# Routing gates of a 16,384-expert layer: one-hot products on TensorE, or accumulating scatters into DRAM

## The chip, the cores and the metric

The kernel runs on one core of one Trainium2 chip. The metric is the device time of one launch in microseconds (us); of several runs the median is taken. Five engines take part: TensorE (PE in the tables, with its weight loads as PEld), VectorE (DVE), ScalarE (ACT), GpSimd (POOL) and SyncE (SP), and 16 DMA engines that move data for all of them. SP, ACT and POOL issue the DMAs.

## The reference, cut to what matters

Two transformer blocks are computed for 256 tokens of width 1024 in float32. The last part is a PEER feed-forward layer: 8 heads, each of which picks 16 of 16,384 experts for each token by a top-16 of two half scores and a top-16 of their 256 sums.

```python
def peer_ffn(xn, w_q, sub_keys, expert_u, expert_v):
    q = (xn @ w_q).reshape(B, S, PEER_HEADS, 2, PEER_QDIM // 2)
    s = jnp.einsum('bshpd,hpkd->bshpk', q, sub_keys)
    v_half, i_half = lax.top_k(s, PEER_TOPK)
    cand = v_half[..., 0, :, None] + v_half[..., 1, None, :]
    top_s, top_c = lax.top_k(cand.reshape(B, S, PEER_HEADS, PEER_TOPK * PEER_TOPK), PEER_TOPK)
    i1 = jnp.take_along_axis(i_half[..., 0, :], top_c // PEER_TOPK, axis=-1)
    i2 = jnp.take_along_axis(i_half[..., 1, :], top_c % PEER_TOPK, axis=-1)
    experts = i1 * PEER_NKEYS + i2
    g = jax.nn.softmax(top_s.astype(jnp.float32), axis=-1)
    ...
        u = expert_u[ec]
        act = jax.nn.gelu(jnp.einsum('cd,ced->ce', xc, u).astype(jnp.float32))
        return jnp.einsum('ce,ced->cd', gc * act, expert_v[ec])
```

Both kernels compute this densely: the activation of every expert for every token, times a dense gate matrix that is zero where an expert was not picked, times all of `expert_v`. Two heads of a token can pick the same expert; their gates add up.

## The kernel before, in words

**The two blocks up to the layer.** Weights come in as 512 KB tiles over SP's queue (`wtile`, lines 236 to 247, four buffers `wf`). A float32 product is done as three products of rounded halves, so each tile is split by ACT (the high part `wh`) and DVE (the low part `wl`). The second block's attention loops over two token tiles `tt` and four head pairs `j` (lines 880 to 909). Then come its output product, a norm, the query product `wq` and the scores `sco` (lines 1010 to 1021). Up to there a planner orders the instructions.

**The u phase (lines 1136 to 1168).** From line 1023 on the order is the program's. The 16,384 experts are 128 columns `i2` of 128 experts. For each of the first `NS` = 122 columns a tile of `expert_u` is loaded by SP (`u_load`), split (`u_low`) and multiplied with the tokens (`u_mm`: 24 products of 256 columns on PE). ACT applies the gelu into one of two buffers (`u_act`) and writes the 128 KB to DRAM (`act_d`, line 1142).

**The routing.** Between the columns DVE does the top-16 steps of `route`, once for each token tile with all 8 heads. The loop keeps two counters of planned DVE and PE time: each column adds 1.2 to DVE's and 2.9 to PE's, and routing steps run while DVE's is the smaller.

**The gates.** When a token tile is routed, PE transposes its indices and gates (`turn`, line 1084). Then for each 4 tokens `g_prep` makes two one-hot tiles on DVE and ACT, `g_mm` multiplies them on PE (line 1120, four products of 128 columns) and `g_evac` copies the result into `gb`, 8 MB for each token tile, on chip (line 1125). That is 64 groups.

**The v phase (lines 1172 to 1255).** The six remaining columns of `expert_u` and the 128 tiles of `expert_v` share one list of jobs. POOL loads the stored activations back, two columns at a time (`act_load`, line 1196), DVE multiplies them with `gb` (line 1205), the product is split, and PE does 12 products of 512 columns for each column (`v_mm`). The tail adds the residual and the last norm.

Of the kernel before, what the change touches and what calls it, by code (L numbers as in the profile page):

```python
# [19 lines left out]
P = 128  # L20
# [12 lines left out]
C_IOTA = C_SIN + 32  # L33
C_I16 = C_IOTA + 128
# [12 lines left out]
def _consts():  # L47
# [12 lines left out]
    c[:, C_IOTA:C_IOTA + P] = np.arange(P)[None, :]  # L60
# [92 lines left out]
def tile_block(ctx, tc, d, out, NS=122, CONV="0.2 0.2 1.1 1.1 1.2", K1=4, M0=7, MR=65, ML=8, MQ=40, WB=3, NTAIL=2, WARM=7):  # L153
# [57 lines left out]
    gt_d = dram.tile([2, D], F32, name="gt_d")  # L211
    cB = xp.tile([P, D], F32, name="cB")
# [475 lines left out]


    with ExitStack() as sb:  # L690
# [4 lines left out]
        cw2 = pb.tile([P, 256], F32, name="cw2")  # L695

# [180 lines left out]
        for tt in range(NT):  # L877
# [3 lines left out]
            for j in range(4):  # L881
# [80 lines left out]
    with ExitStack() as sc_:  # L962
        pc = sc_.enter_context(tc.tile_pool(name="pc", bufs=1))
        act_d = dram.tile([P, P, S], F32, name="act_d")
        iT = pc.tile([P, 2, S], F32, name="iT")
        gT = pc.tile([P, S], F32, name="gT")
        gb = [pc.tile([P, P, P], F32, name="gb0"), None]
        sg_ = ExitStack()
        so = ExitStack()
        po_ = so.enter_context(tc.tile_pool(name="poh", bufs=1, side="right"))  # L970

        def u_prep(i2, lo_eng):
            return wtile(d["u"][i2].rearrange("p a b -> p (a b)"), lo_eng=lo_eng)

        def u_load(i2):
            f = wp.tile([P, 1024], F32, name=nm("wf"), tag="wf", bufs=4)
            nc.sync.dma_start(f, d["u"][i2].rearrange("p a b -> p (a b)"))
# [19 lines left out]
        def u_act(p):  # L997
            a_ = pc.tile([P, S], F32, name=nm("act"), tag="act", bufs=2)
            A.activation(a_, p, AF.Gelu_apprx_tanh)  # L999
            return a_  # L1000
# [23 lines left out]
        i16 = cst[:, C_I16:C_I16 + 16]  # L1024

# [8 lines left out]
        def route(tt, res):  # L1034

            vals = rk.tile([P, 8, 2, 16], F32, name=nm("vals"), tag="vals", bufs=1)
            idx = rk.tile([P, 8, 2, 16], U32, name=nm("idx"), tag="idx", bufs=1)

            def half(h, p_):
                top16(sco[:, tt, h, p_, :], vals[:, h, p_, :], idx[:, h, p_, :], "mr", P)  # L1040

            tv = rk.tile([P, 8, 16], F32, name=nm("tv"), tag="tv")
            ti = rk.tile([P, 8, 16], U32, name=nm("ti"), tag="ti", bufs=1)

            def both(h):
                cand = rk.tile([P, 16, 16], F32, name=nm("cand"), tag="cand")
                V.tensor_tensor(cand, vals[:, h, 0, :, None].to_broadcast([P, 16, 16]),
                                vals[:, h, 1, None, :].to_broadcast([P, 16, 16]), op=OP.add)
                top16(cand.rearrange("p a b -> p (a b)"), tv[:, h, :], ti[:, h, :], "mc", S)

            te = rk.tile([P, 8, 16], F32, name=nm("te"), tag="te")
            idf = rk.tile([P, 8, 2, 16], F32, name=nm("idf"), tag="idf", bufs=1)
            abf = rk.tile([P, 2, 8, 16], F32, name=nm("abf"), tag="abf", bufs=1)
            sel = rk.tile([P, 3, 8, 16], F32, name=nm("sel"), tag="sel")

            def places():
                V.tensor_tensor(te, tv, tv[:, :, 0:1].to_broadcast([P, 8, 16]), op=OP.subtract)
                V.tensor_copy(idf, idx)
                ab = rk.tile([P, 2, 8, 16], U32, name=nm("ab"), tag="ab", bufs=1)
                V.tensor_scalar(ab[:, 0], ti, 4, None, op0=OP.logical_shift_right)  # L1060
                V.tensor_scalar(ab[:, 1], ti, 15, None, op0=OP.bitwise_and)
                V.tensor_copy(abf, ab)
                later.append(lambda: A.activation(te, te, AF.Exp))

            def pick(p_, h4):
                h_ = slice(4 * h4, 4 * h4 + 4)
                e_ = rk.tile([P, 4, 16, 16], F32, name=nm("eq"), tag="eq")
                V.tensor_tensor(e_, abf[:, p_, h_, :, None].to_broadcast([P, 4, 16, 16]),
                                i16[:, None, None, :].to_broadcast([P, 4, 16, 16]), op=OP.is_equal)
                V.tensor_tensor(e_, e_, idf[:, h_, p_, None, :].to_broadcast([P, 4, 16, 16]), op=OP.mult)  # L1070
                V.tensor_reduce(sel[:, p_, h_, :], e_, axis=AX.X, op=OP.add)

            def share():
                zs = rk.tile([P, 8], F32, name=nm("zs"), tag="zs")
                V.tensor_reduce(zs, te, axis=AX.X, op=OP.add)
                V.reciprocal(zs, zs)
                V.tensor_tensor(sel[:, 2], te, zs[:, :, None].to_broadcast([P, 8, 16]), op=OP.mult)
                later.append(turn)

            def turn():  # L1080
                t_ = slice(tt * P, tt * P + P)
                t = gp()[:, 0:384].rearrange("p (i t) -> p i t", i=3)
                for i in range(3):
                    T.transpose(t[:, i, :], sel[:, i].rearrange("p h s -> p (h s)"), ident)
                A.activation(iT[:, :, t_], t[:, 0:2], AF.Copy)
                A.activation(gT[:, t_], t[:, 2, :], AF.Copy)
                res.append(tt)

            for h in range(8):
                for p_ in range(2):  # L1090
                    yield 1.57, lambda h=h, p_=p_: half(h, p_)
            for h in range(8):
                yield 2.75, lambda h=h: both(h)
            yield 1.4, places
            for p_ in range(2):
                for h4 in range(2):
                    yield 3.5, lambda p_=p_, h4=h4: pick(p_, h4)
            yield 0.8, share


        iota = cst[:, C_IOTA:C_IOTA + P]

        def g_prep(t4, mul):

            t_ = slice(4 * t4, 4 * t4 + 4)
            oh = [po_.tile([P, 4, P], F32, name=nm("oh"), tag=f"oh{i}", bufs=2) for i in range(2)]
            for i, o in enumerate(oh):
                V.tensor_tensor(o, iota[:, None, :].to_broadcast([P, 4, P]),
                                iT[:, i, t_, None].to_broadcast([P, 4, P]), op=OP.is_equal)
            if mul is V:  # L1110
                V.tensor_tensor(oh[1], oh[1], gT[:, t_, None].to_broadcast([P, 4, P]), op=OP.mult)
            else:
                for q_ in range(4):
                    A.activation(oh[1][:, q_, :], oh[1][:, q_, :], AF.Copy, scale=gT[:, 4 * t4 + q_:4 * t4 + q_ + 1])
            later.append(lambda: g_mm(t4, oh))

        def g_mm(t4, oh):
            pt = ga_().rearrange("p (t i) -> p t i", t=4)
            for q_ in range(4):
                T.matmul(pt[:, q_, :], oh[0][:, q_, :], oh[1][:, q_, :], start=True, stop=True)  # L1120
            later.append(lambda: g_evac(t4, pt))

        def g_evac(t4, pt):
            tt, o = divmod(4 * t4, P)
            A.activation(gb[tt][:, :, o:o + 4], pt.rearrange("p t i -> p i t"), AF.Copy)


        prep = [u_prep(0, V), u_prep(1, V)]
        later, done = [], []
        gens = iter([route(tt, done) for tt in range(NT)])  # L1130
        cur = next(gens)
        nxt = next(cur)
        g_left = list(range(S // 4))
        dve, pe = 0.0, 0.0
        p = None
        for i in range(NS):
# [11 lines left out]
            if nxt is None and sr is not None and len(done) == NT:  # L1148
                sr.close()
                sr = None  # L1150
                pg1 = sg_.enter_context(tc.tile_pool(name="pg1", bufs=1))
                gb[1] = pg1.tile([P, P, P], F32, name="gb1")

            for n in range(2):
# [161 lines left out]
```

## Time and profile before

| | |
|---|---|
| median of 3 runs | 1244.12 us (1240.11 to 1595.06) |
| the profiled execution | 1238.48 us, span 1236.7 us, mean granted TensorE clock 0.992 |
| PE busy | 1200.8 us, 97% |
| DVE busy | 950.3 us, 77% |
| ACT busy | 699.0 us, 57% |
| POOL busy | 87.6 us, 7% |
| DMA | 264.05 MB, mean 214 GB/s |

The span runs from the first to the last instruction. A busy engine is one with an instruction in flight; products on PE are pipelined, so the busy times of lines can overlap. "Granted clock" is the share of TensorE's full speed.

### The profile page before, as it was taken

The page shows a single profiled execution, that of the slowest core. Times are in us where ns is not written, and L with a number is a line of the kernel's source. Part 1 is how long each engine was busy: PE and PEld are TensorE (multiplying, and loading weights), DVE is VectorE, ACT ScalarE, POOL GpSimd, SP SyncE. Part 2 cuts the span into 40 slices and gives each one's busy share as a digit, 9 for nine tenths or more (in the row PEclk, how much of TensorE's full clock was granted, in tenths as well). Part 3 has the DMA queues.
Part 4 walks back from the last instruction along what each step waited for, and adds up shares of the span by engine and source line. Part 5 has one row for each costly group of instructions (what it writes and reads, how often), then busy time and mean ns, then how long its engine had stood idle before and what let it go on. Part 6 is the DMA issues. An engine that isn't in the chain of part 4 may idle for free.

```text
span 1236.7 us, 20785 instructions
## 1 busy us (share of the span) xinstructions
PE 1200.8 (97%) x7541; PEld 1069.1 (86%) x7541; DVE 950.3 (77%) x1911; ACT 699.0 (57%) x1267; POOL 87.6 (7%) x118
## 2 busy tenths in 40 slices
PE   8999999979988999999999999999999999999996
PEld 7777887879987999999999999999888888888885
DVE  5886969876678589989999899546777777767766
ACT  6566544574455555558878477645444444445443
POOL 2001100010101000000000000000111110101102
PEclk9999999989999999999999999999999999999999
DMA  8876888746523757655555644777776776777764
GB/s 285 301 240 223 292 240 320 262 144 230 187 87 73 251 169 223 224 196 175 182 177 179 208 147 142 230 232 224 242 237 223 238 232 230 230 232 229 241 212 152
DMA packets 86279, 264.05 MB, mean 214 GB/s; under 512 B 10253, under 2 KB 26389, under 8 KB 85664
## 3 DMA queue, kind: packets, MB, share of 16 engines
q1 hardware_dynamic: 62352, 225.03, 55.6%
q0 software_dynamic: 5680, 19.48, 5.0%
q10 hardware_dynamic: 18144, 18.23, 4.2%
q8 instruction: 59, 0.97, 0.3%
q14 instruction: 44, 0.36, 0.1%
HBM read 244.58 MB, written 19.68 MB: 214 GB/s over the span
## 4 chain that ended last, share of the span: by engine, by line
PE 79%; issue 7%; DVE 7%; DMA 3%; ACT 2%; POOL 1%; SPq 0%; ACTq 0%; POOLq 0%; DVEq 0%
PE sc L994 9%; PE sc L992 9%; PE sc L993 9%; PE po L1230 5%; PE pg L1230 5%; PE po L1229 5%; PE po L1231 5%; PE pg L1229 5%; PE pg L1231 5%; PE pg L1120 5%; PE pg L257 3%; PE pg L258 3%; PE pg L256 3%; DVE wl L231 2%; DMA wf<-in_w_br_dram 2%
## 5 line engine op out<-in xcount | busy, mean ns | idle before, releaser
L231 DVE TENSOR_TENSOR wl<-wf,wh 128x1024 fp32r<-128x1024 f32 (+3 forms) x255 | 302.5, 1189 | 131.7 <-ACT wh L230 131.3
L230 ACT ACTIVATE wh<-wf 128x1024 fp32r<-128x1024 f32 (+3 forms) x255 | 260.1, 1022 | 119.4 <-PE pg L258 49.2
L992 PE MATMUL sc<-hThi,wh 128*128 128x256 f32 x1024 | 293.8, 287 | 0.0
L994 PE MATMUL sc<-hThi,wl 128*128 128x256 f32 x1024 | 290.7, 284 | 2.3 <-DVE wl L984 2.3
L993 PE MATMUL sc<-hTlo,wh 128*128 128x256 f32 x1024 | 289.5, 283 | 0.0
L994 PEld LDWEIGHTS sc<-hThi,wl 128*128 128x128 f32 x1024 | 196.0, 191 | 3.8 <-DVE wl L984 2.9
L993 PEld LDWEIGHTS sc<-hTlo,wh 128*128 128x128 f32 x1024 | 196.3, 192 | 0.2
L992 PEld LDWEIGHTS sc<-hThi,wh 128*128 128x128 f32 x1024 | 196.1, 192 | 0.2
L984 DVE TENSOR_TENSOR wl<-wf,wh 128x1024 fp32r<-128x1024 f32 x122 | 147.7, 1217 | 49.4 <-ACT wh L979 48.7
L230 ACT ACTIVATE wwh<-w 128x256 fp32r<-128x256 f32 x128 | 53.4, 417 | 170.7 <-issue 147.6
L979 ACT ACTIVATE wh<-wf 128x1024 fp32r<-128x1024 f32 x122 | 128.9, 1057 | 31.5 <-ACT act L999 18.6
L256 PE MATMUL pg<-wh,hThi 128*128 128x512 f32 (+1 forms) x264 | 102.2, 388 | 1.9 <-ACT hThi L323 1.9
L257 PE MATMUL pg<-wl,hThi 128*128 128x512 f32 (+1 forms) x264 | 102.6, 389 | 0.4 <-DVE wl L231 0.4
L1230 PE MATMUL po<-wl,wwh 128*128 128x512 f32 x256 | 102.1, 399 | 0.0
L1230 PE MATMUL pg<-wl,wwh 128*128 128x512 f32 x256 | 102.1, 399 | 0.0
L258 PE MATMUL pg<-wh,hTlo 128*128 128x512 f32 (+1 forms) x264 | 102.1, 388 | 0.0
L1229 PE MATMUL po<-wh,wwh 128*128 128x512 f32 x256 | 100.9, 394 | 0.0
L1229 PE MATMUL pg<-wh,wwh 128*128 128x512 f32 x256 | 100.9, 394 | 0.0
L1231 PE MATMUL po<-wh,wwl 128*128 128x512 f32 x256 | 100.4, 392 | 0.0
L1231 PE MATMUL pg<-wh,wwl 128*128 128x512 f32 x256 | 100.3, 392 | 0.0
L1196 POOL DMA_DIRECT2D actl<-act_d x61 | 44.2, 725 | 746.4 <-ACT act L999 378.9
L999 ACT ACTIVATE act<-sc 128x256 f32<-128x256 f32 x128 | 48.1, 376 | 75.8 <-PE sc L994 71.8
(375 smaller groups left out, 2122.4 us busy)
## 6 DMA issues: line engine op xcount, KB each, us to landing
wf<-in_u_dram SPq DMA_DIRECT2D x128, 512.0 KB, 3.8
wf<-in_v_dram SPq DMA_DIRECT2D x128, 512.0 KB, 4.2
wf<-in_w_in_dram SPq DMA_DIRECT2D x68, 512.0 KB, 5.2
wm<-in_w_mod_dram SPq DMA_DIRECT2D x48, 512.0 KB, 6.1
act_d<-act ACTq DMA_DIRECT2D x122, 128.0 KB, 3.3
actl<-act_d POOLq DMA_DIRECT2D x61, 256.0 KB, 4.3
wf<-in_w_out_dram SPq DMA_DIRECT2D x16, 512.0 KB, 4.8
wf<-in_w_br_dram SPq DMA_DIRECT2D x8, 512.0 KB, 10.5
```

Source lines behind the costliest of these rows:

```text
L230: A.activation(hi, src, AF.Copy)
L231: (lo_eng or V).tensor_tensor(lo, src, hi.bitcast(F32), op=OP.subtract)
L256: T.matmul(p, lh[:, k, t], hh, start=first, stop=False)
L257: T.matmul(p, lh[:, k, t], l_, start=False, stop=False)
L258: T.matmul(p, ll[:, k, t], hh, start=False, stop=last)
L984: V.tensor_tensor(l, f, h.bitcast(F32), op=OP.subtract)
L992: T.matmul(p, h[:, o], hThi[:, k, :], start=(k == 0), stop=False)
L993: T.matmul(p, h[:, o], hTlo[:, k, :], start=False, stop=False)
L994: T.matmul(p, l[:, o], hThi[:, k, :], start=False, stop=(k == KD - 1))
L1229: T.matmul(pO[tt][n], wh[:, t_], h[:, c_], start=first, stop=False)
L1230: T.matmul(pO[tt][n], wh[:, t_], l[:, c_], start=False, stop=False)
L1231: T.matmul(pO[tt][n], wl[:, t_], h[:, c_], start=False, stop=last)
```

## The change

The dense gate matrix moves from the chip to DRAM, and the activations from DRAM to the chip.

- A DRAM tensor `g_d` of 128 x 128 x 256 floats (16.8 MB) is filled with zeros by 32 writes of 512 KB on ACT's queue, four after each `j` step of the second block's attention.
- The routing goes by groups of heads, (0), (1), (2, 3), (4, 5), (6, 7), both token tiles in a group. At the end of a group the cell numbers are computed, and for each row (a head and a token tile) POOL issues 16 indirect DMAs, each of which adds 128 gates of 4 bytes, one for each token, into `g_d`. The first transfer of a row waits until the 16 of the same token tile one head earlier have landed; nothing else orders them. That is 256 transfers.
- `g_prep`, `g_mm`, `g_evac`, `turn` and `act_d` are gone. The gelu writes into activations that stay on chip, 80 columns in one tile and 48 in a second, made where the routing's buffers were. All 128 columns of `expert_u` run in the u phase.
- When the routing is over, POOL queues loads of the gates, two columns (256 KB) at a time, three buffers. The first waits until the transfers of the last head have landed. `w_make` multiplies activations and gates, one DVE instruction for 256 tokens instead of two for 128. `w_make(0)` stands in the u phase ahead of the split of the tile that is loaded at column 126.

```diff
+    g_d = dram.tile([P, P, S], F32, name="g_d")
+    g_flat = g_d.rearrange("i p (t o) -> (i p t) o", o=1)
...
+    def zero_gates(zero, n):
+        return nc.scalar.dma_start(g_d.rearrange("i p t -> i (p t)")[:, 1024 * n:1024 * n + 1024].rearrange("i (a b) -> i a b", b=512),
+                            zero[:, None, :].to_broadcast([P, 2, 512]))
...
                 for k, at in enumerate(CONV.split()):
                     if at == f"{tt}.{j}":
                         conv[k]()
+                for n in range(4):
+                    tc.keep_in_program_order(zero_gates(zero, 16 * tt + 4 * j + n))
...
+        acts = [pc.tile([P, NA, S], F32, name="act0"), None]
+        ixr = pc.tile([P, 16, 16], U32, name="ixr")
+        gtr = pc.tile([P, 16, 16], F32, name="gtr")
...
-        for tt in range(NT):
-            for h2 in range(4):
+        for h2 in range(4):
+            for tt in range(NT):
...
-        man = sc_.enter_context(tc.manual_schedule())
+        man = sc_.enter_context(tc.manual_schedule(engines={getattr(mybir.EngineType, e) for e in ("PE", "DVE", "Activation", "SP")}))
...
+        def scatter(r):
+            h, tt = divmod(r, NT)
+            for j in range(16):
+                q_ = nc.gpsimd.indirect_dma_start(g_flat, bass.IndirectOffsetOnAxis(ap=ixr[:, r, j:j + 1], axis=0),
+                                                  gtr[:, r, j:j + 1], None, compute_op=OP.add)
+                prev = scat.get(r - NT, []) if j == 0 else []
+                for o_ in prev:
+                    tc.add_manual_dep(q_.ins, o_.name, mybir.DependencyInfo(mybir.DependencyClass.Sync,
+                                                                        mybir.DependencyReason.DATA),
+                                      reason="a head after the one before")
+                tc.declare_no_dep(q_.ins, group="scat", keep=prev, reason="other cells, or a later wait")
...
+            def cells():
+                f = rk.tile([P, 4, 16], F32, name=nm("cf"), tag="cf")
+                V.scalar_tensor_tensor(f[:, :n], sel[:, 1, :n], float(P * S), tok[:, :n, None].to_broadcast([P, n, 16]),
+                                       op0=OP.mult, op1=OP.add)
+                V.scalar_tensor_tensor(ixr[:, R], sel[:, 0, :n], float(S), f[:, :n], op0=OP.mult, op1=OP.add)
 
             def share():
...
-                later.append(turn)
-
-            def turn():
...
+                for r in range(r0, r0 + n):
+                    scatter(r)
...
-        def g_prep(t4, mul):
...
-        def g_mm(t4, oh):
...
-        def g_evac(t4, pt):
...
+        steps = (st_ for heads in ((0,), (1,), (2, 3), (4, 5), (6, 7)) for st_ in route(heads))
...
+        def g_load():
+            if g_todo:
+                i2 = g_todo.pop(0)
+                g_ = pw.tile([P, 2, S], F32, name=nm("gl"), tag="gl", bufs=3)
+                q_ = nc.gpsimd.dma_start(g_, g_d[i2:i2 + 2].rearrange("i p t -> p i t"))
+                if i2 == 0:
+                    for r in (14, 15):
+                        for o_ in scat[r]:
...
+                                              reason="all gates are in")
...
+        def w_make(i2):
+            w = pw.tile([P, S], F32, name=nm("w"), tag="w", bufs=2)
+            V.tensor_tensor(w, act_of(i2), gls.pop(i2), op=OP.mult)
+            if i2 % 2:
+                g_load()
...
+        for i in range(P):
             now, later = later, []
             q = p
             p = u_mm(*prep.pop(0))
             if q is not None:
-                nc.scalar.dma_start(act_d[i - 1], u_act(q))
+                A.activation(act_of(i - 1), q, AF.Gelu_apprx_tanh)
...
+            if i == P - 2:
+                w_make(0)
...
             prep.append(u_low(*h))
+            if nxt is None and pw is None:
+                sr.close()
+                pa_ = sg_.enter_context(tc.tile_pool(name="pa1", bufs=1))
+                acts[1] = pa_.tile([P, P - NA, S], F32, name="act1")
+                pw = sg_.enter_context(tc.tile_pool(name="pw", bufs=1, side="right"))
+                for _ in range(3):
+                    g_load()
+        A.activation(act_of(P - 1), p, AF.Gelu_apprx_tanh)
+        w_make(1)
...
+        for i in range(P):
             h, l = prep.pop(0)
-            if kind == "u":
-                acts[i2] = u_act(u_mm(h, l))
-                continue
...
+            if i + 2 < P:
+                w_make(i + 2)
+                prep.append(u_low(*u_load(P + i + 2)))
```

## Rows read from the trace of the kernel before

**Rows 1.** First parts of the page: busy time of each engine, and PE in 40 slices.

```profile
PE 1200.8 (97%) x7541; PEld 1069.1 (86%) x7541; DVE 950.3 (77%) x1911; ACT 699.0 (57%) x1267; POOL 87.6 (7%) x118
PE   8999999979988999999999999999999999999996
```

**Rows 2.** Windows: length; busy us of PE, PEld, DVE, ACT, POOL; clock, DMA share, GB/s.

```profile
460.00:480.00 20.00, 20.00 (x169) 20.00 (x168) 18.92 (x66) 10.11 (x14) 0.00 (x0) 1.00 0.72 226
500.00:550.00 50.00, 49.10 (x408) 48.68 (x407) 43.99 (x68) 26.19 (x37) 0.00 (x0) 1.00 0.67 223
650.00:700.00 50.00, 49.14 (x412) 48.72 (x410) 47.40 (x71) 34.24 (x61) 0.00 (x0) 1.00 0.61 194
800.00:850.00 50.00, 50.00 (x419) 50.00 (x418) 21.20 (x18) 25.14 (x35) 0.00 (x0) 1.00 0.77 230
900.00:1000.00 100.00, 100.00 (x442) 81.01 (x441) 72.58 (x141) 48.92 (x72) 12.31 (x17) 1.00 0.72 232
```

**Rows 3.** Chain that ended last, in the u phase: start, length, what.

```profile
548.93 1.29 DVE oh L1108 x2
...
628.07 0.89 PE pg L1120 x8
631.83 0.89 PE pg L1120 x8
...
775.00 1.78 PE pg L1120 x16
779.65 1.78 PE pg L1120 x16
```

**Rows 4.** Lines L1142, L1120, L1084: shortest/median/longest ns, first and last start.

```profile
L1142 ACTq DMA_DIRECT2D act_d<-act x121: 326/327/362, 440.6 to 848.1; - x121
L1120 PE MATMUL pg<-oh,oh x512: 270/275/347, 551.2 to 781.2; 128*128 128x128 f32 x171
L1084 PE MATMUL pg<-cst,sel x6: 270/272/272, 548.0 to 706.3; 128*128 128x128 f32 x6
```

**Rows 5.** Groups of POOL by line and form: busy us, mean ns of one, idle before.

```profile
L1196 POOL DMA_DIRECT2D actl<-act_d x61 | 44.2, 725 | 746.4 <-ACT act L999 378.9 <-DVE w L1205 286.1 <-DMA wf<-in_v_dram 68.3
L371 POOL DMA_DIRECT2D gt_d<-modc x2 | 1.9, 964 | 34.4 <-DVE modc L366 34.4
L499 POOL DMA_DIRECT2D rel<-in_rel_dram x1 | 0.5, 545 | 0.0
```

**Rows 6.** DMA issues over the whole span: count, KB each, median us to landing.

```profile
wf<-in_u_dram SPq DMA_DIRECT2D x128, 512.0 KB, 3.8
actl<-act_d POOLq DMA_DIRECT2D x61, 256.0 KB, 4.3
gt_d<-modc POOLq DMA_DIRECT2D x2, 4.0 KB, 10.8
e<-e__989 POOLq DMA_DIRECT2D x1, 12.0 KB, 2.8
```

**Rows 7.** DMA totals of the stretches 170:178, 397:400, 400:403 and 181:184.

```profile
DMA packets 181, 0.60 MB, mean 75 GB/s; under 512 B 35, under 2 KB 35, under 8 KB 181
...
DMA packets 20, 0.08 MB, mean 27 GB/s; under 512 B 0, under 2 KB 0, under 8 KB 20
...
DMA packets 22, 0.09 MB, mean 30 GB/s; under 512 B 0, under 2 KB 0, under 8 KB 22
...
DMA packets 332, 1.27 MB, mean 422 GB/s; under 512 B 23, under 2 KB 23, under 8 KB 332
```

**Rows 8.** DMAs issued between 397 and 400: count, KB each, median us to landing.

```profile
wf<-in_wq_dram SPq DMA_DIRECT2D x1, 512.0 KB, 10.3
```

**Rows 9.** Window of the second block's attention, columns as in the windows above.

```profile
340.00:400.00 60.00, 54.06 (x351) 47.03 (x349) 46.51 (x109) 31.57 (x75) 4.77 (x9) 1.00 0.30 82
```

More of the change, by code (lines that the diff above doesn't have):

```diff
@@ L695, in tile_block @@
         cw2 = pb.tile([P, 256], F32, name="cw2")
+        zero = pb.tile([P, 512], F32, name="zero")
+        G.memset(zero, 0.0)
         def proj_T(ci, consume):
@@ L995, in u_mm, with act_of @@
             return p
[L997 to L1000, printed above, removed]
+        def act_of(i2):
+            return acts[0][:, i2, :] if i2 < NA else acts[1][:, i2 - NA, :]
         sr = ExitStack()
@@ L1090, in route @@
                 for p_ in range(2):
[L1091 to L1094, printed above, removed]
+                    yield 1.57, lambda r=r, p_=p_: half(r, p_)
+            for r in range(n):
+                yield 2.75, lambda r=r: both(r)
+            yield 1.2, places
             for p_ in range(2):
-                for h4 in range(2):
-                    yield 3.5, lambda p_=p_, h4=h4: pick(p_, h4)
+                yield 0.9 * n, lambda p_=p_: pick(p_)
@@ L1098, in route @@
+            yield 0.5, cells
             yield 0.8, share
-        iota = cst[:, C_IOTA:C_IOTA + P]
-        def g_prep(t4, mul):
[L1105 to L1115, printed above, removed]
@@ L1131, in tile_block @@
-        cur = next(gens)
-        nxt = next(cur)
-        g_left = list(range(S // 4))
+        prep = [u_low(*u_load(0)), u_low(*u_load(1))]
+        steps = (st_ for heads in ((0,), (1,), (2, 3), (4, 5), (6, 7)) for st_ in route(heads))
+        nxt = next(steps)
         dve, pe = 0.0, 0.0
         p = None
-        for i in range(NS):
+        gls, g_todo = {}, list(range(0, P, 2))
+        pw = None
+        wts = {}
+        def g_load():
[6 more added lines that the diff above has]
+                        for o_ in scat[r]:
+                            tc.add_manual_dep(q_.ins, o_.name, mybir.DependencyInfo(mybir.DependencyClass.Sync,
+                                                                                mybir.DependencyReason.DATA),
+                                              reason="all gates are in")
+                    keep = [o_ for r in (14, 15) for o_ in scat[r]]
+                else:
+                    keep = []
+                tc.declare_no_dep(q_.ins, group="scat", keep=keep, reason="the first load waited for all")
+                tc.stamp_issue_order_token(q_.ins, "gates")
+                gls[i2], gls[i2 + 1] = g_[:, 0, :], g_[:, 1, :]
@@ L1138, in tile_block @@
+        def w_make(i2):
[3 more added lines that the diff above has]
+                g_load()
+            wh = pw.tile([P, S], F32R, name=nm("wwh"), tag="wwh", bufs=4)
+            wl = pw.tile([P, S], F32R, name=nm("wwl"), tag="wwl", bufs=4)
+            split(w, wh, wl)
+            wts[i2] = (wh, wl)
+        for i in range(P):
             now, later = later, []
@@ L1147, in tile_block @@
             pe += 2.9
[L1148 to L1154, printed above, removed]
-                if g_left and gb[g_left[0] // 32] is not None and g_left[0] // 32 in done and (n == 0 or nxt is None):
-                    g_prep(g_left.pop(0), V if n else A)
-                    dve += 1.8 if n else 1.2
-                    pe += 0.88
+            if i == P - 2:
+                w_make(0)
             while nxt is not None and dve < pe:
@@ L1161, in tile_block @@
                 nxt[1]()
-                nxt = next(cur, None)
-                if nxt is None:
-                    cur = next(gens, None)
-                    nxt = next(cur) if cur else None
+                nxt = next(steps, None)
             prep.append(u_low(*h))
-        nc.scalar.dma_start(act_d[NS - 1], u_act(p))
-        assert not g_left and not later
-        so.close()
-        pO = [[op_(), op_()], [gp(), gp()]]
-        pw = sg_.enter_context(tc.tile_pool(name="pw", bufs=1, side="right"))
@@ L1175, in tile_block @@
-        seq = []
-        ls, lu = list(range(NS)), list(range(NS, P))
-        seq = [lu.pop(0), lu.pop(0)]
-        n1, n2 = len(ls) - 6, len(lu)
-        for i in range(n1 + n2):
-            seq.append((lu if (i + 1) * n2 // (n1 + n2) > i * n2 // (n1 + n2) else ls).pop(0))
-        seq += ls
-        assert not lu
-        jobs = []
-        for i in range(P + 2):
-            if i < P and seq[i] >= NS:
-                jobs.append(("u", seq[i]))
-            if i >= 2:
-                jobs.append(("v", seq[i - 2]))
```

166 lines of the change are left out of this document (54 added, 112 removed).

## The prediction

> **What bounds the kernel now.** I read the page's busy times first: PE is busy 97% of the span and 90% or more in nearly every slice [rows 1]. The windows then say where another engine could matter: at 800 to 850 and at 900 to 1000 PE has no gap, while in the routing (460 to 480) DVE stands at 18.9 of 20 us and PE still has no gap [rows 2]. So in the u phase and in the v phase the time is the sum of PE's work; what leaves PE there is gained, unless something else comes late.
>
> The chain gives PE's price of each step. With one gate group per column, groups stand 3.76 us apart and take 0.89; with two, 4.65 apart and 1.78. Both leave 2.87 us for one column of `u_mm` [rows 3]. The first activation is stored at 440.6 [rows 4], so the u phase begins about one column and a gelu earlier, at 437.
>
> **The change part by part.**
>
> *Gates off PE.* 64 groups by 0.89 us [rows 3] are 57.0 us, all on PE, in a phase where PE has no gap. The six transposes of `turn` take at most 0.27 us each [rows 4] and are pipelined: 1 us. Gain 58.0 us. The one-hot work on DVE and ACT and the copies into `gb` go too; both were hidden under PE, so they count nothing.
>
> *Six columns moved from the v phase to the u phase.* The same 2.87 us each on PE in either place: 0. Their loads stay on SP's queue, one per column.
>
> *Routing in five groups.* The instructions are those of before on smaller tiles plus two for the cell numbers in each group, a few us of DVE in all; the counters spread it over more columns, and DVE's last 5% of slack in the routing [rows 2] covers it. Without that cover it would cost PE what it is longer. The exponent, though, now runs five times instead of twice between gelus, and each time PE lost about 0.9 us (49.10 and 49.14 of 50) [rows 2]: plus 2.7 us.
>
> *The pace of the routing.* The planned costs are 17.9 for a group of two rows and 33.3 for one of four, 135.6 in all, at 2.9 - 1.2 = 1.7 per column: groups end at columns 10.5, 21, 41, 60 and 80. The old order bears this out: its first 63.3 make 37 columns, 437 + 107 = 544, and the first one-hots come at 549 [rows 3]. With 3 us for the zero fill (below) the groups end at 470, 500, 557, 613 and 672.
>
> *The zero fill.* 16.8 MB at 422 GB/s, the fullest stretch that I read [rows 7], are 40 us of all DMA engines. In the attention (340 to 400) they are busy 0.30 of the time [rows 9], so 42 us are free there. ACT issues 32 writes at 0.33 us as before for its stores [rows 4], 10.5 us where ACT is idle half the time. If all of it fits: 0. If weights for the output product and `wq` queue behind what does not fit, up to 20 us. I take 3, near the free end, because the free time is as long as the fill.
>
> *Stores and loads.* 16 MB of activation stores go. The gate loads have the size, the engine and the count of the old activation loads (64 by 256 KB for 61), about 0.73 us of POOL each and 4.3 to landing [rows 5, 6]; nothing on the path as long as the first is in time. In the v phase DVE does less and PE the same: 0.
>
> *The deadline of the scatters.* The u phase ends at 440 + 128 x 2.87 + 5 x 0.9 = 812. `w_make(0)` stands two columns ahead of it on DVE, at 806. If the first gate load has not landed then, DVE waits, the split of the next weight tile is queued behind it, and PE runs dry. Less 4.3 us for the load and 2.8 for the last landing (the 12 KB transfer) [rows 6], the last scatter must be issued by 799. The row-to-row wait costs nothing: 16 other transfers are issued between, more than 10 us at any price below, against a landing of 2.8 to 10.8 [rows 6].
>
> *What a scatter costs POOL.* No indirect transfer is in the trace. Its ends: 0.55 us, the smallest direct DMA on POOL, and 1.93, twice the 0.96 of the DMA with 1024 pieces of 4 bytes [rows 5], because an accumulate may need two descriptors per piece. I take 1.0, by the 4-byte row. Then the last issue is at 557 + 192 x 1.0 = 749: 50 us early. The price at which the deadline falls is (799 - 557) / 192 = 1.26.
>
> *What a scatter costs the DMA engines.* The nearest row is that same DMA, `gt_d`: 4 KB, which land after 10.8 us [rows 6]. While it is in flight, weights hardly move: 0.60 MB in the 8 us from 170, 0.17 MB in the 6 us from 397 [rows 7], and a `wq` tile takes 10.3 us to land against 3.8 for a u tile [rows 6, 8]. At 422 GB/s those bytes need 1.4 and 0.4 us, so 1024 small writes took 6.6 and 5.6 us from the weights, 0.70 to 0.82 us for 128. The ends: nothing at all, if cells far apart do not get in each other's way as 4 KB side by side may; and 1.64, twice the upper value, if the accumulate's read costs as much as its write. A gain is excluded, since a transfer is only added. I take 0.75, the rows' middle. From 470 to 806 are 336 us; 117 weight tiles of 0.524 MB take 145 of them at 422 GB/s, which leaves 191 for 256 scatters, 0.75 each. So it just fits, with no reserve.
>
> What the traces show here, lost bandwidth under 4-byte writes, is also a rule: the Trainium skill, "DMA: Bandwidth & Descriptors", section "Specifications", wants 512 bytes per piece, below which the engine reads, modifies and writes. The rows agree. The page's section on measured transfers has 0.68 us for 4 KB over 128 partitions; by that figure, as an estimate for one scatter, the sum would stay as it is.
>
> *Sum.* 1238.5 (the profiled execution) - 58.0 + 2.7 + 3 = 1186. That execution lies 5.6 us below the median of the three runs, 1244.1, and 1.6 below the lowest; with half of the 5.6 added I forecast **1189 us**, 4.4% faster. No change (within 2%, about what a measurement of this kernel can tell) is 1219 to 1269, that is a stall of 30 to 80 us.
>
> **The rivals.**
>
> *DMA engines too slow for the scatters: the weights starve.* Place: the u phase from 470 on. Stall: 256 x price - 191. It decides at 0.75; at 0.86 it is no change, from 1.06 on slower. At the doubled 1.64 it is 229 us, 1418. For it: the `gt_d` rows lie right at the edge [rows 7], and an accumulate reads too. Against it: `gt_d` packs all its pieces into 4 KB and hands each DMA engine 64 in one go, a scatter 8. Chance 0.24: 0.09 no change, 0.15 slower.
>
> *POOL too slow to issue them.* Stall: the later of 470 + 256 x price and 557 + 192 x price, less 799. At 1.40 us it is 30, at 1.60 it is 80, at 1.93 it is 165: 1354. For it: an indirect transfer must read 128 offsets first, and nothing in the trace prices that. Against it: 1024 pieces cost POOL only 0.96 us, 256 cost 0.73, one small DMA 0.55, so pieces are cheap [rows 5]. Chance 0.20: 0.06 no change, 0.14 slower.
>
> *One landing at a time.* If each accumulate in effect waits for the one before, 256 landings of 2.8 us [rows 6] are 717 us; the last is at 1187, a stall of 388: 1577. Against it: the change lets the 16 transfers of a row go unordered. Chance 0.04. The Trainium skill, the same page, "Anatomy of one DMA", puts about 2.0 us of fixed cost on each POOL transfer, most of it in waiting for the receipt, and its rules advise against many small ones; no run here shows 256 in a row, and with 2.0 in place of 2.8 the estimate would be 1372.
>
> *The zero fill collides.* With 16.8 MB behind the attention's weights at 20 to 40 us instead of 3, the time is 1206 to 1226. Against it: the 42 us of free DMA time [rows 9]. Chance 0.04, half of it within 2%.
>
> *The gates leave PE and nothing follows*, because DVE or ACT, freed of one-hots but with a shorter phase, now sets the column: about 1240. Against it: without gate groups and routing DVE is busy 21 of 50 us and PE keeps its 2.87 [rows 2, 3]. Chance 0.02.
>
> **How the numbers follow.** The forecast, a stall below 30 us, has the rest, 0.46, and its own range is 1175 to 1219. Faster: 0.46 and half of the zero fill, 0.48. No change: 0.09 + 0.06 + 0.02 + 0.02 = 0.19. Slower: 0.15 + 0.14 + 0.04 = 0.33. The overall range goes from 1175 (all terms at their good ends, and runs as low as the profiled one) to 1310, a stall of 121 us: a DMA price of 1.22 or a POOL price of 1.76. Beyond it I leave 0.06 of the first rival, 0.06 of the second, the serial landings, and 0.04 below.
>
> **What would show it.** L1120 gone and u columns 2.87 us apart: the gain is real. A POOL scatter of at most 1.26 us, and POOL's first gate load issued before 802: the deadline holds. DVE's product in `w_make(0)` waiting for a DMA at the end of the u phase: a scatter rival; then POOL busy without gaps from 470 on says issue, and u tiles that land after far more than 3.8 us, with PE gaps all through the u phase, say DMA engines. Late tiles before 440 say zero fill. The prediction is wrong in its core if a scatter costs over 1.26 us on POOL or takes over 0.75 us from the weights.

## The result, and the profile after

The changed kernel takes **1438.11 us** (median of 4 runs, 1436.72 to 1440.12) against 1243.15 for the kernel before: 1.158 times as long (95% interval 1.155 to 1.160). One of the four runs of the kernel before, 1595.06 us, was a slow one and is left out of the ratio. The forecast was 1189, its range ended at 1310. The forecast is wrong. The time lies above what the prediction gave for POOL at its upper price (1354) and for starving weights at the doubled one (1418), and below serial landings (1577).

The profiled execution is 1436.72 us with a span of 1434.8, 198.1 more than before. First the page's busy times and three of its 40-slice rows, which answer to [rows 1]:

```profile
PE 1171.8 (82%) x7023; PEld 1007.2 (70%) x7023; DVE 860.8 (60%) x1679; ACT 607.0 (42%) x1016; POOL 563.7 (39%) x378
...
PE   9999999898889999999999800000099999999996
...
POOL 2001000101000588888888888888611111111112
PEclk9999999999999999999999955555599999999999
```

PE does less work than before, but six slices are empty, and in these POOL goes on as in the slices before them: it has one long run of work, from slice 14 to slice 29. The windows answer to [rows 2, 9]; columns as there.

```profile
340.00:360.00 20.00, 15.63 (x98) 14.84 (x99) 15.28 (x38) 6.86 (x17) 0.98 (x1) 0.83 1.01 352
340.00:400.00 60.00, 51.17 (x318) 44.48 (x319) 39.35 (x95) 27.32 (x64) 4.58 (x7) 0.94 0.84 294
...
500.00:550.00 50.00, 50.00 (x419) 50.00 (x419) 47.15 (x134) 25.43 (x38) 42.99 (x24) 1.00 0.76 183
650.00:700.00 50.00, 49.97 (x415) 49.69 (x415) 36.26 (x56) 25.58 (x38) 43.29 (x23) 1.00 0.75 187
700.00:750.00 50.00, 50.00 (x419) 50.00 (x418) 21.64 (x18) 22.68 (x34) 44.51 (x19) 1.00 0.69 185
...
900.00:950.00 50.00, 0.00 (x0) 0.00 (x0) 0.00 (x0) 0.00 (x0) 41.83 (x27) 0.50 0.23 0
...
1000.00:1100.00 100.00, 61.56 (x247) 46.55 (x248) 42.38 (x65) 29.37 (x45) 36.40 (x31) 0.79 0.52 140
1100.00:1200.00 100.00, 100.00 (x402) 72.79 (x401) 66.27 (x100) 45.56 (x67) 11.38 (x17) 1.00 0.70 222
```

Three things are to be seen. At 500 to 750 PE has no gap while POOL issues. At 900 to 950 only POOL works: 27 transfers in 50 us, 1.85 each, of which 41.83 / 27 = 1.55 busy. And POOL's count for 50 us is not the same everywhere: 27 with the others idle, 19 at 700 to 750. The v phase does 402 products in 100 us where it did 442 [rows 2]; 24 of the 442 belong to a column of `expert_u`, which lay in that window, so 402 stand against some 418 in 97 us.

What PE waits for is in DVE's list of waits (line waited for; us in total, times, longest) and in the chain of the stretch from 800 to 1045, of which these are among the longest pieces (start, length, what):

```profile
DVE w L1154 <- DMA gl<-g_d: 223.6, 1, 223.6
```

```profile
803.31 2.58 POOL g_d L1046
...
811.95 2.58 POOL g_d L1046
1029.93 2.98 DMA g_d<-gtr,ixr
1033.46 3.23 DMA gl<-g_d
```

One wait of 223.6 us: the first product of gates and activations, for the first gate load, which POOL could issue at 1033.5 only. The groups and one line of POOL, against [rows 4, 5] (busy, mean ns, idle before; then shortest, median, longest ns, first and last start):

```profile
L1046 POOL DMA_INDIRECT g_d<-gtr,ixr x256 | 473.6, 1850 | 142.7 <-issue 77.4
...
L1137 POOL DMA_DIRECT2D gl<-g_d x64 | 45.6, 713 | 322.5 <-DVE w L1154 308.2
```

```profile
L1046 POOL DMA_INDIRECT g_d<-gtr,ixr x256: 1548/1550/2592, 480.1 to 1029.9; - x128
...
  issue: 77.4, 254
  DMA wf<-in_u_dram: 65.0, 1
  DVE zs L1106: 0.3, 1
```

From the first start to the end of the last the 256 transfers take 551 us, **2.154 us each**. Of POOL's idle time before them 77.4 us are 0.30 between one transfer and the next, and the routing (`zs`) was waited for 0.3 us, once: after the first transfer POOL was never short of gates. DMA issues and their landing, against [rows 6]:

```profile
wf<-in_u_dram SPq DMA_DIRECT2D x128, 512.0 KB, 3.7
...
g_d<-zero ACTq DMA_DIRECT2D x32, 512.0 KB, 7.5
gl<-g_d POOLq DMA_DIRECT2D x64, 256.0 KB, 3.9
```

u tiles land in 3.7 us (3.8 before): 256 accumulating transfers beside them cost the weights nothing that these rows show. Each u column is one gelu of ACT, and these follow one another at 2.88 us, as the bare column of [rows 3] (timeline of ACT in the u phase):

```profile
599.67 0.38 ACT L1167 ACTIVATE act<-sc 128x256 f32<-128x256 f32 x1 [1.55 <-PE sc L1000]
...
602.55 0.38 ACT L1167 ACTIVATE act<-sc 128x256 f32<-128x256 f32 x1 [1.55 <-PE sc L1000]
```

**Where the 198.1 us are.** First u and v products start at 436.9 and 856.1 before; after, at 449.4 and 1037.6, and the last u product stands at 818.6. So the u phase begins 12.5 late; PE stands still for 218.7 (818.9 to 1037.6); and the rest from the first u product to the end is 799.8 before against 985.4 - 218.7 = 766.7 after, 33.1 less. 12.5 + 218.7 - 33.1 = 198.1. The 33.1 hold the gain of 58 and a loss that the experiments size.

### The profile page after: what moved, and what is told of

The parts are those of the page before. It is cut to its first block, busy times and chain, and to the rows that moved or that the text cites. A ratio compares the mean times of both kernels' runs of the same rounds, so it can differ in the third digit from the quotient of the medians.

```text
span 1434.8 us, 19082 instructions
## 1 busy us (share of the span) xinstructions
PE 1171.8 (82%) x7023; PEld 1007.2 (70%) x7023; DVE 860.8 (60%) x1679; ACT 607.0 (42%) x1016; POOL 563.7 (39%) x378
## 4 chain that ended last, share of the span: by engine, by line
PE 54%; POOL 25%; issue 11%; DVE 5%; ACT 3%; DMA 2%; SPq 0%; POOLq 0%; DVEq 0%; ACTq 0%
POOL g_d L1046 24%; PE po L1197 6%; PE po L1198 4%; PE pg L1196 4%; PE po L1196 4%; PE pg L1197 4%; PE pg L1198 4%; PE sc L1000 4%; PE sc L998 4%; PE sc L999 4%; PE pg L259 3%; PE pg L260 3%; PE pg L258 3%; DVE wl L233 1%; DMA wf<-in_w_br_dram 1%
## 5 line engine op out<-in xcount | busy, mean ns | idle before, releaser
L1046 POOL DMA_INDIRECT g_d<-gtr,ixr x256 | 473.6, 1850 | 142.7 <-issue 77.4
L990 DVE TENSOR_TENSOR wl<-wf,wh 128x1024 fp32r<-128x1024 f32 x256 | 312.0, 1223 | 156.6 <-ACT wh L985 156.2
L998 PE MATMUL sc<-hThi,wh 128*128 128x256 f32 x1024 | 290.5, 284 | 0.0
L985 ACT ACTIVATE wh<-wf 128x1024 fp32r<-128x1024 f32 x256 | 268.2, 1048 | 3.6 <-PE pg L304 3.6
L1196 PEld LDWEIGHTS po<-wh,wwh 128*128 128x128 f32 x256 | 48.4, 189 | 231.6 <-ACT wwh L232 218.7
L1154 DVE TENSOR_TENSOR w<-act,gl 128x256 f32<-128x256 f32 x128 | 53.5, 418 | 223.6 <-DMA gl<-g_d 223.6
L1137 POOL DMA_DIRECT2D gl<-g_d x64 | 45.6, 713 | 322.5 <-DVE w L1154 308.2
L233 DVE TENSOR_TENSOR wl<-wf,wh 128x1024 fp32r<-128x1024 f32 (+3 forms) x121 | 138.0, 1150 | 45.9 <-ACT wh L232 45.6
L232 ACT ACTIVATE wh<-wf 128x1024 fp32r<-128x1024 f32 (+3 forms) x121 | 119.7, 995 | 99.5 <-PE pg L260 50.4
L1197 PE MATMUL po<-wl,wwh 128*128 128x512 f32 x256 | 114.2, 446 | 1.6 <-DVE wl L990 1.6
```

The lines of the kernel that those rows point to most:

```text
L232: A.activation(hi, src, AF.Copy)
L233: (lo_eng or V).tensor_tensor(lo, src, hi.bitcast(F32), op=OP.subtract)
L990: V.tensor_tensor(l, f, h.bitcast(F32), op=OP.subtract)
L998: T.matmul(p, h[:, o], hThi[:, k, :], start=(k == 0), stop=False)
L1046: q_ = nc.gpsimd.indirect_dma_start(g_flat, bass.IndirectOffsetOnAxis(ap=ixr[:, r, j:j + 1], axis=0), gtr[:, r, j:j + 1], None, compute_op ...
L1196: T.matmul(pO[tt][n], wh[:, t_], h[:, c_], start=first, stop=False)
```

## The experiments

The disputed point is what one scatter costs, and whom. My theory after the result: POOL's issue is the bound, at 1.55 us of its own plus 0.30, stretched by DVE while weights are split; DMA engines and landings don't set the end. Rivals: the DMA engines; a landing that is waited for; the routing. Beside it stand 12.5 us ahead of the u phase and the slower v phase.

**Half of the transfers.**

```diff
-            for j in range(16):
+            for j in range(0, 16, 2):
```

> Every second transfer of each row is left out (128 of 256; the other gates stay zero, so the result is not the reference's). If POOL's issue price of 2.15 us sets the end, 128 transfers end near 690 to 800, before the first gate load is due at about 816: the 216 us of waiting go, 1438 - 216 = about 1222, and POOL has idle time between the groups. If the DMA engines or one landing at a time set it, the price per transfer is the same and so is this time; those are told apart by the next two. If the wait came from something else (the loads, the zero fill), more than 50 us of it stay.

Measured: 1216.98 us, 0.982 of before (0.980 to 0.984). The scatters end at 805, the first gate load goes out at 811, and the v products follow the u products without a gap (line of u products, then of v products: ns, first and last start):

```profile
L998 PE MATMUL sc<-hThi,wh x1024: 281/283/468, 451.1 to 820.3; 128*128 128x256 f32 x171
```

```profile
L1196 PE MATMUL po<-wh,wwh x256: 388/396/502, 820.7 to 1200.8; 128*128 128x512 f32 x128
```

The stall is a matter of the number of transfers, and the deadline lies where the prediction put it (806 plus the late start). Without a stall the change would still be 28 us short of the forecast; the fill and the v phase, sized below, are what is left.

**The same without the addition**, that is plain writes: where two heads pick one expert the later gate replaces the earlier.

```diff
-                                                  gtr[:, r, j:j + 1], None, compute_op=OP.add)
+                                                  gtr[:, r, j:j + 1], None)
```

> The transfers write instead of adding (a cell hit by two heads keeps one gate). If the price is POOL's issue of one indirect instruction, nothing moves: 1.55 us alone, 2.15 with the gaps and the collisions, 1438 us. If the accumulate's second access costs POOL or the DMA engines, the price falls: at half of 1.85 us the stall is gone and the time is about 1222.

Measured: 1477.75 us in one run, and neither theory had that. On POOL a plain transfer is cheap, but the u phase now lasts from 451.1 to 1079.9 (line of the scatters; a window of that phase; PE's waits from 480 to 960, columns as in DVE's list above):

```profile
L1046 POOL DMA_INDIRECT g_d<-gtr,ixr x256: 955/962/1993, 481.9 to 957.5; - x128
```

```profile
900.00:950.00 50.00, 16.04 (x49) 12.44 (x49) 3.68 (x3) 3.16 (x5) 38.12 (x40) 0.50 0.11 31
```

```profile
PE sc L1000 <- issue: 62.2, 54, 3.1
PE sc L999 <- issue: 57.1, 52, 3.1
PE sc L998 <- issue: 56.8, 58, 2.4
PE sc L1000 <- DVE wl L990: 0.2, 1, 0.2
```

Two things follow. A plain scatter takes POOL 0.96 us, so the addition is 1.55 - 0.96 = 0.59 of the price. And while plain scatters are issued PE falls behind, and the weights come at 31 GB/s. That looks like the rival of starving weights, but it is not: for a weight tile, by way of its split on DVE, PE waits 0.2 us in these 480. The other 176 us are gaps of up to 3.1 us between its own products, put down to "issue", that is to nothing that the profile shows. A tile that is asked for is soon there (SP's timeline, then the DMA totals of 910 to 915):

```profile
911.77 0.33 SPq L983 DMA_DIRECT2D wf<-in_u_dram  x1
```

```profile
DMA packets 268, 0.53 MB, mean 105 GB/s; under 512 B 140, under 2 KB 140, under 8 KB 268
```

The 0.52 MB of the tile have moved by 915, at most 3.2 us after its issue. So few weights move because PE uses few. Why PE's products start so late beside plain scatters and not beside adding ones is not shown and stays open. The transfers are cut differently: POOL's queue moves 3888 / 27 = 144 packets for each adding transfer (900 to 950 in the kernel after) and 80 for one of 64 cells (next run), which fits one for each cell and 16 more; for each plain one it moves 8192 / 256 = 32, so several cells in one packet.

**64 cells in each transfer instead of 128**, half of the tokens' gates left out.

```diff
-   ap=ixr[:, r, j:j + 1]
-   gtr[:, r, j:j + 1], None, compute_op=OP.add
+   ap=ixr[0:64, r, j:j + 1]
+   gtr[0:64, r, j:j + 1], None, compute_op=OP.add
```

> Each transfer carries the cells of partitions 0 to 63 alone (the gates of the other tokens stay zero). A price per instruction: 1.55 us stays and the time is 1438. A price per cell, on POOL or on the DMA engines: 0.8 us or less, no stall, about 1222. A mixture shows its two parts: price = a + 128 b against a + 64 b.

Measured: 1376.54 us, one run; scatters from 484.1 to 970.2, v products from 977.5. In the stretch without other work (850 to 900):

```profile
850.00:900.00 50.00, 0.00 (x0) 0.00 (x0) 0.00 (x0) 0.00 (x0) 41.02 (x30) 0.50 0.16 0
```

41.02 / 30 gives 1.37 with the cut ones at the ends, 1.41 by the median of whole ones, against 1.55: half the cells save 0.14 us. If the price is a line through these two points, which two points can't show, 2.2 ns belong to each cell and 1.27 us to the instruction. With the gap of 0.30 even an empty one would be at 1.57, over the deadline's 1.26: smaller transfers would not have met it, fewer would. Packets alone don't set the price: here they fall from 144 to 80 and 0.14 us go, without the addition from 144 to 32 and 0.59 go. The records don't tell what POOL does within its 1.55 us.

**DVE against POOL.** In the stall, 24 each of four DVE operations on 512 columns, in this order: two inputs added, one reduced, top-8 of one, one copied.

```diff
+                for _ in range(24):
+                    V.tensor_tensor(sc_r, a0, b0, op=OP.add)
...
+                    V.tensor_reduce(sc_r[:, 0:8], ..., axis=AX.X, op=OP.add)
...
+                    V.max(sc_r[:, 0:8], a0)
...
+                    V.tensor_copy(sc_r, a0)
```

> While POOL alone works (after the u phase), DVE runs four blocks of 24 instructions on 512 columns each: TENSOR_TENSOR with two SBUF inputs, TENSOR_REDUCE, MAX8, and a float32 copy. If POOL's 2.57 us in the u phase is a wait for DVE's two-input split, transfers beside the first block are longer than 1.55 us and beside TENSOR_REDUCE and MAX8 they stay at 1.55; the copy can go either way. If it is the DMA traffic of the weights that lengthens them, all four blocks leave 1.55 us, for no weights move then. The time is 1438 to 1460 us.

Measured: 1440.64 us, one run. POOL's timeline (start, length; the blocks begin at 813.5, 831.0, 848.3 and 865.8, the copies end at 878.3):

```profile
821.76 1.87 POOL L1046 DMA_INDIRECT g_d<-gtr,ixr  x1 [0.30 <-issue]
...
838.22 1.55 POOL L1046 DMA_INDIRECT g_d<-gtr,ixr  x1 [0.30 <-issue]
...
854.91 1.55 POOL L1046 DMA_INDIRECT g_d<-gtr,ixr  x1 [0.31 <-issue]
...
872.13 1.80 POOL L1046 DMA_INDIRECT g_d<-gtr,ixr  x1 [0.30 <-issue]
...
880.29 1.55 POOL L1046 DMA_INDIRECT g_d<-gtr,ixr  x1 [0.30 <-issue]
```

Beside additions of two tiles a transfer takes 1.87, beside copies 1.80, beside reductions and top-8 searches, of which DVE does as much, 1.55 as alone. From about 820 on no weights move and PE is idle, so it is DVE's kind of operation that stretches POOL's. In the u phase the operation is above all the split of a weight tile, `wl = wf - wh`, two inputs of 1024 columns. The timelines of the kernel after (POOL, then DVE) show when it stretches a transfer:

```profile
598.93 1.55 POOL L1046 DMA_INDIRECT g_d<-gtr,ixr  x1 [0.30 <-issue]
...
614.53 2.01 POOL L1046 DMA_INDIRECT g_d<-gtr,ixr  x1 [0.30 <-issue]
...
690.99 2.58 POOL L1046 DMA_INDIRECT g_d<-gtr,ixr  x1 [0.30 <-issue]
```

```profile
599.13 1.21 DVE L990 TENSOR_TENSOR wl<-wf,wh 128x1024 fp32r<-128x1024 f32 x1
...
613.89 1.23 DVE L990 TENSOR_TENSOR wl<-wf,wh 128x1024 fp32r<-128x1024 f32 x1 [1.08 <-ACT wh L985]
...
690.91 1.23 DVE L990 TENSOR_TENSOR wl<-wf,wh 128x1024 fp32r<-128x1024 f32 x1 [1.65 <-ACT wh L985]
```

The first transfer begins ahead of a split and takes 1.55, though the split then runs beside it. The second begins within one and ends at 616.54, 1.42 us after the split does; so does the third. That is the rule in all 256: 100 begin while a two-input operation of DVE runs, 98 of these end some 1.42 us after that operation, and they hold 76.7 of the 76.8 us by which the transfers exceed 1.55 each. So a transfer waits for the operation that it finds running, and is not slowed by later ones. From about 680 on POOL falls into step: each transfer begins 0.08 us into a split and lasts 2.57, 2.88 with the gap, just one u column. The pace of POOL is DVE's there. The Trainium skill, "SBUF — State Buffer", section "SBUF: two separate sides", has a lock that DVE and GpSimd share: a DVE operation with two inputs in that memory, or an fp32 copy in it, shuts GpSimd out while it runs, and transfers from GpSimd's queue then look blocked. Both kinds that stretch a transfer here are among those that it names, and the two that don't are not, so the traces agree. Its example is 0.62 us alone and 3.1 beside a copy; here it is 1.55 and 1.80. What is waited for is at most the rest of one operation, so of the 16 us from 814 to 830, 15.25 of them busy on DVE, POOL still got eight transfers.

**The v product one column ahead**, as in the kernel before, with half of the transfers so that no stall hides it.

```diff
+        def w_mul(i2):
+            ws[i2] = pw.tile([P, S], F32, name=nm("w"), tag="w", bufs=2)
+            V.tensor_tensor(ws[i2], act_of(i2), gls.pop(i2), op=OP.mult)
...
             if i + 2 < P:
+                if i + 3 < P:
+                    w_mul(i + 3)
                 w_make(i + 2)
```

> As e1 (128 of 256 transfers left out), and in the v phase each column's product of activation and gate is made one column ahead, so that ACT's rounding of it no longer waits for DVE. If the 2.99 us of a v column (2.80 before) come from that wait, it goes back to 2.80 and the time from 1217 to 1217 - 128 x 0.19 = 1193. If the gate loads or the DMA traffic set 2.99, nothing moves.

Measured: 1192.04 us, 0.962 of before (0.960 to 0.965); the half alone had 0.982, so the order is worth 2.0%, 25 us (both leave out half of the gates). In the 100 us from 900 on it does 431 v products, the kernel after 402 from 1100 on, and PE counts as busy for 100.00 us in both: the count shows the loss, the busy time doesn't. The reason stands in the timelines of the kernel after (first fence) and before (second), at the start of a v column:

```profile
1149.51 0.42 DVE L1154 TENSOR_TENSOR w<-act,gl 128x256 f32<-128x256 f32 x1
...
1149.96 0.42 ACT L232 ACTIVATE wwh<-w 128x256 fp32r<-128x256 f32 x1 [1.62 <-DVE w L1154]
...
1152.95 0.42 ACT L232 ACTIVATE wwh<-w 128x256 fp32r<-128x256 f32 x1 [1.63 <-DVE w L1154]
```

```profile
951.16 0.49 DVE L1205 TENSOR_TENSOR w<-actl,gb 128x128 f32<-128x128 f32 x2
951.42 0.42 ACT L230 ACTIVATE wwh<-w 128x256 fp32r<-128x256 f32 x1 [1.43 <-issue]
...
954.22 0.42 ACT L230 ACTIVATE wwh<-w 128x256 fp32r<-128x256 f32 x1 [1.43 <-issue]
```

Before, ACT's rounding starts while DVE still makes the product of the next column (951.42 against 951.16 + 0.49); after, it waits for the product of its own column, which DVE makes behind the split of the weight tile. ACT and DVE then take turns in one chain of 2.99 us, and PE, with 2.80 us of work, waits for it. 128 x 0.19 = 24 us.

**The zero writes on POOL's queue**, beside that.

```diff
-        return nc.scalar.dma_start(g_d...
+        return nc.gpsimd.dma_start(g_d...
```

> As e5, with the 32 zero writes issued by POOL instead of ACT. If the u phase starts 12.5 us late because ACT stands still while its queue takes the writes (2.7 to 3.4 us for four), 8 to 12 us of it go: about 1183. If the 16.8 MB themselves hold up the weights, nothing moves: 1193. POOL's own issue of 0.6 to 0.8 us each may hold up its few steps of the attention by some us.

Measured: 1188.23 us (0.958, interval 0.956 to 0.959), first u product at 449.6 against 450.2. The 8 to 12 us did not come, but the run is inconclusive: the queue changes little, but POOL's own step of the norm (L854) also moved, from 338.5 to 348.1 us. Three kernels without scatters tell bytes from issues.

**No fill, a small fill, the whole fill.** All three load their gate tiles from another tensor.

```diff
 (the first)  -  tc.keep_in_program_order(zero_gates(zero, 16 * tt + 4 * j + n))
 (the second) -  [:, 1024 * n:1024 * n + 1024]
              +  [:, 1024 * n:1024 * n + 64]
```

> The kernel after without any of its 256 scatters and without the zero fill; the gate tiles are loaded from another DRAM tensor of the right size, so the gates are not computed. Read at the first matmul of the u phase, which was at 436.9 us in the kernel before and at 449.4 in the kernel after. If the zero fill is what delays it: about 437 to 440. If something else of the change does (the routing's order, the staged values): 448 to 450. The time itself, with no scatter to wait for and 2.99 us per column in the v phase: about 1205, since the half with 128 scatters took 1217.

> The same, with 32 zero writes issued by ScalarE as in the kernel after, each of one sixteenth of the bytes; gates are again not computed. First matmul of the u phase: if the bytes of the fill cost the delay, about 437 to 440, as without it; if the 32 issues on ScalarE's queue cost it, about 448 to 450.

> The same, with the full zero fill and no scatter; gates are again not computed. The control of the two kernels beside it: first matmul of the u phase at about 449, and a time about 12 us above the one without a fill, if the fill is the whole of the delay.

Measured, one run each: 1210.53, 1211.02 and 1219.77 us; first u product at 441.4, 441.8 and 450.5. The first two missed their 437 to 440, the first also its 1205, and the third is 9.2 us longer than the first instead of 12. The first was late before any zero write could be: the same product of the second block (line 825 before, 834 after), just ahead of the fill's place, starts at

```profile
L825 PE MATMUL po<-vbd,ct x4: 590/592/594, 310.1 to 311.4; 128*128 128x512 f32 x4
```

```profile
L834 PE MATMUL po<-vbd,ct x4: 592/592/592, 314.4 to 315.7; 128*128 128x512 f32 x4
```

in the kernel before (310.1) and in that without a fill (314.4), whose granted clock at 300 to 320 was 0.83 where before had 1.00. From that product to the first u product it is 126.8 us before, 127.0 without a fill, 441.8 - 312.8 = 129.0 with the small one, 139.4 with the whole one and 449.4 - 309.7 = 139.7 in the kernel after. So within these single runs the fill is the whole of the delay: 32 small writes cost 2.0 us, the bytes 10.4 more.

**A version with less of it.** In the kernel before, token tile 1 alone gets its gates by 128 scatters, into 8.4 MB; tile 0 keeps the one-hot products, and the v phase its order. The second kernel also issues the zero writes on POOL.

```diff
-        gens = iter([route(tt, done) for tt in range(NT)])
+        gens = iter([route_s(h_) for h_ in ((0, 1), (2, 3), (4, 5, 6, 7))] + [route(0, done)])
...
-            for tt in range(NT):
-                t_ = slice(tt * P, tt * P + P)
-                V.tensor_tensor(w[:, t_], a_[:, t_], gb[tt][:, i2, :], op=OP.mult)
+            V.tensor_tensor(w[:, 0:P], a_[:, 0:P], gb[0][:, i2, :], op=OP.mult)
+            V.tensor_tensor(w[:, P:S], a_[:, P:S], gls.pop(i2), op=OP.mult)
```

> The kernel before, with token tile 1's gates alone built by scatters (128 transfers, all gates present, 8.4 MB of zeros written by ACT) and tile 0's by one-hot products as before; activations go through DRAM as before. 32 gate groups of 0.89 us leave PE: 28.5 us; the zero fill costs half of 12.5, four exponents instead of two 1.8: 1239 - 28.5 + 6 + 2 = about 1218. By POOL's price (2.15 us, and up to 5 us for each of seven waits from head to head) the scatters end by 475 + 275 + 35 = 785, ahead of the end of the u phase at about 825: no wait. If the scatters were slower than that, DVE waits at the first product of the v phase and the time is above 1239.

> As e7, with the 16 zero writes issued by POOL. If ACT's queue is what the fill costs, about 6 us less than e7: 1212. If the bytes cost it, the same as e7.

Measured: 1214.57 us, 0.979 of before (0.977 to 0.981), and 1212.39, 0.978 (0.975 to 0.980). The scatters stand at 475.5 to 770.0, the first v product at 832.9: no stall, half of the gate groups gone (32 x 0.89 = 28 us) and 7.1 of it given back to the late start (444.0). With POOL issuing, the u phase starts at 441.5 and 2.2 us go, where 6 or none were expected; the intervals overlap. Both kernels hold all gates and stand below both kernels of the case, but against the kernel before only by the 2% that the prediction took as about what a measurement of this kernel can tell.

## Why the prediction was wrong, point by point

- **"What a scatter costs POOL" is the step that failed**, by its size: 1.0 taken, ends 0.55 and 1.93, decided at 1.26; it measured 2.154. The parts: 0.96 for the plain transfer; 0.59 for the addition; 0.30 between one instruction and the next, which no busy time of [rows 5] holds and which I left out; 0.30 on the mean from DVE's two-input operations, above all the splits. That the 0.96 is the value of the 4-byte row is luck as far as the runs show: the row's transfer has 1024 pieces, the scatter 128. The upper end doubled 0.96 for the addition and left out the other two; no run shows that an addition needs two descriptors per piece. Even alone, at 1.85, a scatter misses the deadline.
- "The deadline of the scatters" held. With 2.154 in its formula, (557 + 192 x 2.154) - 799 or 470 + 256 x 2.154 - 799, the stall is 172 or 222; 218.7 were measured, with the first scatter at 480.1 and the deadline 12.5 later. POOL never waited for gates after the first, so the second form applies: the rival "POOL too slow to issue them" is what happened, at a chance of 0.20 and priced at 1354. With 2.154 for its 1.93 it would have said 1189 + 222 = 1411; the fill and the v phase make up about the rest.
- "What a scatter costs the DMA engines" failed the other way: 0.75 taken, nothing measured (u tiles in 3.7 us, PE 50.00 of 50). Plain transfers, of the kind of its row, don't show it either: beside them PE waits 0.2 us for weights. The 260 us by which the plain kernel's u phase is longer lie in PE's own gaps, whose cause is open, and in the low clock that goes with them (0.50 at 900 to 950).
- "One landing at a time" is out: with the others idle a transfer lands after 3.0 us and the next follows after 1.85. The page of the Trainium skill named there, "DMA: Bandwidth & Descriptors", section "Anatomy of one DMA", has about 2.0 us fixed on each transfer, near the measured pace; but by the trace 1.55 of it are POOL's own work, not a wait for a receipt.
- "The zero fill" was taken at 3 and cost 12.5 (2.0 issues, 10.4 bytes); the rival "the zero fill collides" is this one, small. The free DMA time of [rows 9] was counted over 60 us, but the writes came in clumps: at 340 to 360 DMA has a share of 1.01 and PE 15.63 of 20 us, at 340 to 400 DMA 0.84 and PE 51.17 instead of 54.06.
- "Stores and loads" was taken at 0 for the v phase and cost 24 us: DVE does less, but the product is no longer made a column ahead, and a chain took the place of PE as the bound. The prediction counted busy time and did not follow who waits for whom.
- "Gates off PE" was right: L1120 is gone and u columns are 2.88 us apart. "Six columns moved", "The pace of the routing" and its cover were right too. From the first u product to the end, less the empty stretch, 33.1 us were gained: 58 less 24, and less about 2.7 for the slower clock after the stall (397.2 us from the first v product to the end against 394.5 in the half), leave 31; the 2 us between are not assigned. The exponents' 2.7 don't show: PE has 49.97 us of 50 or more in the windows of the u phase from 500 to 750.

## What to carry to other kernels

Many small transfers are priced first by their issuing engine: count x (instruction + gap), with what its neighbour does to it when it begins, against the moment when the last must be in. A row of another kind of transfer prices neither the addition nor the neighbour. A low rate of weights is no proof that weights are short: look at what the engine that uses them waits for. And a step that loses work can still become slower if it is no longer made ahead: follow the chain of who waits, not only the busy time.

## What the runs showed of the hardware

- POOL's accumulating scatter of 128 cells of 4 bytes: 1.55 us and 0.30 to the next; 64 cells 1.41; plain 0.96. Beside DVE's two-input operations or fp32 copies of 512 columns 1.87 and 1.80, in step with splits of 1024 columns 2.57: a transfer that begins within a two-input operation ends 1.42 us after it (98 of 100).
- Beside plain scatters (32 packets each) PE's products started late, with 176 us of gaps from 480 to 960 that no recorded wait explains; beside accumulating ones (144 packets) PE had no gap. Neither kind is seen to hold the weights up.
- The granted clock stood at 0.50, the 1.2 GHz level, while PE was idle (830 to 1037). PE began again at 1037.6, and from 1043 on the clock was at 1.00; the v phase took some 2.7 us longer than in the half.
